# A hybrid Hyena, attention and expert block on one core: the conditioning with its weights as stationary operand, filter norms summed by TensorE, and x times root in place

## The chip, the core and the metric

One NeuronCore of a Trainium2 chip, one launch. The metric is the device time of one execution in microseconds, as the median of several runs. The core has TensorE (PE in the profile; its weight loads are shown as PEld), VectorE (DVE), ScalarE (ACT), GpSimd (POOL) and SyncE (SP, which issues most DMAs). Each engine takes its own instructions in order.

## What is computed

All in float32, on x of 512 tokens by 1024, a context of 256 tokens, and two condition vectors c and c_ctx. Cut to what matters here:

```python
m_lat = silu(c) @ w_ada + b_ada          # 6 modules of 1024
m_ctx = silu(c_ctx) @ w_ada + b_ada
sh1, sc1, g1, sh2, sc2, g2 = m_lat       # of m_ctx only the first two are used
h = rmsnorm(x, norm1_g) * (1 + sc1) + sh1
h_ctx = rmsnorm(ctx, norm1_g) * (1 + cs1) + ch1
# hyena: two long filters, made by a small network with sines and a decay
filt = mlp(positions) * decay            # [512, order 2, forward/backward, 512]
filt = filt / sum(abs(filt))             # over positions and both directions
z = h @ w_in + b_in                      # 5120 columns: hyena 1536, q, k, v, two gates
zc = cw[0] * z[t-1] + cw[1] * z[t] + cw[2] * z[t+1] + conv_b     # the hyena columns
y_hy = hyena(zc, filt)                   # long convolutions through a Fourier transform
x1 = x + g1 * ((gate1 * (y_hy @ w_hy_out) + gate2 * (attention(h, h_ctx) @ w_na_out)) @ w_out)
out = x1 + g2 * experts(rmsnorm(x1, norm2_g) * (1 + sc2) + sh2)
```

The experts are 16384 rows of two tables, of which each token and head takes 16.

## The kernel before

The kernel is one long program written with a tile framework: the Python code gives the work in a rough order, and the framework puts each engine's instructions into a fixed order by a simulated time line. `issue_after` ties an instruction's place to another's.

Matrices whose precision matters are split into a high and a low part (`split`, L202 to L211: ACT copies the high part, DVE or GpSimd subtracts it), and each product is made of three (`mm3`, L221; `project`, L227). A product of plain float32 operands leaves two records of matmul in the trace; one of split operands leaves one.

The part that the change touches is the opening, `run`, L819 to L866:

- `conditioning` (L335) makes the first two modules (shift and scale of the first norm), for c and c_ctx at once. For each of 8 blocks of 128 inputs it loads two 128x1024 pieces of `w_ada` (L352; the first module's into the buffers of later weight splits, `wh`/`wl`, two each, the second module's into five buffers `wada`). The first module goes to TensorE with the two condition columns as the stationary operand (128x2) and 512 weight columns moving, summed in PSUM over the blocks (L347). The second module does so for blocks 5 to 7 only; for blocks 0 to 4 (SIDE = 5) DVE multiplies the piece by the condition's value of each partition and adds it to two accumulators `raw` of 128x1024 (L356, L358), which TensorE folds in at the end of block 6 by products with a column of ones (L364). The two rows of each module, over four PSUM banks of the tag "s", are copied to SBUF (L370, L371), turned into columns by 16 small transposes (L373), and the bias is added (L374); L377 makes the scale.
- `rstd` (L413) sums the squares of x (ACT squares, GpSimd adds), transposes, takes the root and spreads it back over the partitions (L403 to L419).
- `modulate` (L422) makes the normalised input: for each of 8 blocks x times root (L427), times scale plus shift (DVE L431 or ACT L429 in turns), and the split (low part on DVE or GpSimd in turns).
- `filter_mlp` (L239) is the small network; `filters` (L260) makes one long filter, for two orders, `f0` and `f1`. For each of four blocks of 128 positions: two products (L282), times decay (L284), magnitude by ACT into one of two buffers `fd` (L286), the larger of the two (L289 or L295), and, from the second block on, GpSimd adds it to `l1` (L296). In the first block, one row of the first position is added, halved and copied by DVE (L291 to L293). Then the filter is split, TensorE sums `l1` over the partitions (L304, with 128 columns of `l1` as the stationary operand and two columns of ones moving), and `spectrum` (L314) makes its transform from PSUM banks "s" (four of them). The transform's matrix `dft` (2 MB) is fetched on GpSimd's queue after the squares are summed (L841).
- `hy_block` (L487) is one block of projection and short convolution: 24 products, ACT adds the bias (L493), then DVE takes the middle tap with its bias (L494) and adds the two others (L495, L496). Four of its twelve calls are in the opening, eight in `hyena`.

Weights go through three buffers `raw`; the fetch of the first projection weights stands behind the last fetch of the conditioning (`hold`, L846). The conditioning is a generator, resumed between the steps of the filter network.

Behind the opening come the Hyena convolutions with gates (to about 300 us), attention (to about 550 us), the output projection, and the experts (routing, then all expert columns for three quarters of the tokens with a one-hot spread, and gathered rows for the others) to the end.

## Time and profile before

| | us |
|---|---|
| Median of 3 runs | 1899.73 |
| Lowest and highest run | 1883.78, 1901.09 |
| Profiled execution | 1897.7 |
| Its span, first to last instruction | 1895.9 |
| PE busy | 1818.9 (96%) |
| DVE busy | 1469.6 (78%) |
| ACT busy | 839.8 (44%) |
| POOL busy | 543.5 (29%) |
| Moved by DMA | 429.37 MB, mean 226 GB/s |

Times in the rows are microseconds from the span's start. A busy PE is not a PE at its peak: matmuls are pipelined, and the duration of one is longer than the distance to the next. The granted clock is the share of TensorE's 2.4 GHz. In a row that merges several instructions the duration runs from the first start to the last end.

### The profile page before, as it was taken

To read this page: it belongs to the slowest core of one execution; us is meant where nothing else is said; L and a number is where in the kernel's file an instruction comes from. 1 tells how busy PE (TensorE), PEld (TensorE's weight loads), DVE (VectorE), ACT (ScalarE), POOL (GpSimd) and SP (SyncE) were. 2 spreads that over 40 slices of the span, in tenths; PEclk is the share of its full clock that TensorE was granted. 3 is DMA by queue.
4 is the path that set the end of the run, shared out by engine and by line. 5 is a ranking of instruction groups with operands and counts; after the bars stand their busy time and mean duration, and the time that the engine had idled before them with its cause. 6 is when DMAs were issued, how large, how long until landed. Compare 5 with 4: busy or idle time off the path is not lost.

```text
span 1895.9 us, 26957 instructions
## 1 busy us (share of the span) xinstructions
PE 1818.9 (96%) x9939; PEld 1569.0 (83%) x9939; DVE 1469.6 (78%) x2741; ACT 839.8 (44%) x1278; POOL 543.5 (29%) x377
## 2 busy tenths in 40 slices
PE   6899999999999899999999999999999999999997
PEld 1578887878877788899998988889999999987876
DVE  7879865665788688877995768787777877778987
ACT  2553334545554543346886333333333333333332
POOL 3440000000002333340000444444444444433440
PEclk8999999999999999999999999999999999999999
DMA  8443323333477422245668979989998888889995
GB/s 306 134 164 108 123 86 120 115 110 97 133 272 239 128 84 79 79 133 190 259 263 296 320 272 331 324 305 327 323 322 301 317 318 306 302 280 333 333 329 198
DMA packets 167933, 429.37 MB, mean 226 GB/s; under 512 B 14999, under 2 KB 70487, under 8 KB 163832
## 3 DMA queue, kind: packets, MB, share of 16 engines
q1 hardware_dynamic: 127656, 280.82, 43.8%
q0 software_dynamic: 40144, 146.82, 21.2%
q8 instruction: 78, 1.28, 0.3%
q14 instruction: 55, 0.45, 0.1%
HBM read 387.22 MB, written 38.27 MB: 224 GB/s over the span
## 4 chain that ended last, share of the span: by engine, by line
PE 67%; DVE 13%; DMA 8%; issue 6%; POOL 2%; ACT 2%; SPq 1%; ACTq 0%; DVEq 0%; POOLq 0%
PE a L233 26%; PE a L235 13%; PE s L223 5%; PE s L224 5%; PE s L225 5%; POOL row L1282 2%; PE t L225 2%; PE t L223 2%; PE t L224 2%; DMA row<-in_u_rows,ei 2%; DMA raw<-in_v_rows 1%; DMA wada<-in_w_ada 1%; DMA row<-in_v_rows,ei 1%; PE s L1268 1%; PE s L1269 1%
## 5 line engine op out<-in xcount | busy, mean ns | idle before, releaser
L233 PE MATMUL a<-h,wh 128*128 128x384 f32 (+1 forms) x2944 | 613.6, 358 | 5.3 <-ACT ring L1032 1.3
L233 PEld LDWEIGHTS a<-h,wh 128*128 128x128 f32 x2944 | 524.7, 190 | 52.1 <-issue 1.9
L204 ACT ACTIVATE wh<-raw 128x1024 fp32r<-128x1024 f32 (+1 forms) x208 | 213.7, 1027 | 369.6 <-DMA raw<-in_u_cols 180.8
L235 PE MATMUL a<-h,wl 128*128 128x384 f32 (+1 forms) x1472 | 318.5, 354 | 0.0
L1282 POOL DMA_INDIRECT row<-in_u_rows,ei x128 | 186.1, 1454 | 403.1 <-DVE row L1287 387.0
L235 PEld LDWEIGHTS a<-h,wl 128*128 128x128 f32 x1472 | 261.6, 188 | 17.5
L205 DVE TENSOR_TENSOR wl<-raw,wh 128x1024 fp32r<-128x1024 f32 (+1 forms) x173 | 203.5, 1176 | 75.7 <-ACT wh L204 37.1
L1282 POOL DMA_INDIRECT row<-in_v_rows,ei x128 | 185.0, 1445 | 246.5 <-DVE h2n L1296 217.7
L1287 DVE SCALAR_TENSOR_TENSOR row<-row,h2n 128x1024 f32<-128x1024 f32 x128 | 154.9, 1222 | 69.7 <-DMA row<-in_u_rows,ei 69.5
L224 PE MATMUL s<-vl,wsh 128*128 128x512 f32 x512 | 200.8, 393 | 7.1 <-DVE vl L205 6.9
L225 PE MATMUL s<-vh,wsl 128*128 128x512 f32 x512 | 198.9, 391 | 0.0
L204 ACT ACTIVATE wsh<-w 128x384 fp32r<-128x384 f32 x128 | 67.0, 523 | 267.6 <-PE t L224 156.1
L223 PE MATMUL s<-vh,wsh 128*128 128x512 f32 x512 | 176.4, 391 | 6.1 <-ACT vh L204 3.0
L1296 DVE SCALAR_TENSOR_TENSOR h2n<-row,dots,h2n 128x1024 f32<-128x1024 f32 x127 | 162.6, 1281 | 19.5 <-DMA row<-in_v_rows,ei 18.7
L205 DVE TENSOR_TENSOR vl<-raw,vh 128x1024 fp32r<-128x1024 f32 x128 | 156.1, 1220 | 8.3 <-ACT vh L204 8.3
L204 ACT ACTIVATE vh<-raw 128x1024 fp32r<-128x1024 f32 x128 | 134.6, 1052 | 39.0 <-DMA raw<-in_v_rows 33.2
L443 POOL DMA_DIRECT2D yv<-in_w_ada x32 | 17.2, 536 | 380.8 <-DVE yv L453 165.2
L205 POOL TENSOR_TENSOR wl<-raw,wh 128x1024 fp32r<-128x1024 f32 x35 | 85.0, 2431 | 124.9 <-PE a L235 116.5
L224 PEld LDWEIGHTS s<-vl,wsh 128*128 128x128 f32 x512 | 96.6, 189 | 28.0 <-DVE vl L205 10.9
L223 PEld LDWEIGHTS s<-vh,wsh 128*128 128x128 f32 x512 | 95.8, 188 | 24.8 <-ACT vh L204 4.8
L205 DVE TENSOR_TENSOR wsl<-w,wsh 128x384 fp32r<-128x384 f32 x128 | 71.1, 555 | 55.8 <-ACT wsh L204 53.7
L225 PEld LDWEIGHTS s<-vh,wsl 128*128 128x128 f32 x512 | 96.8, 189 | 19.8
(361 smaller groups left out, 2982.2 us busy)
## 6 DMA issues: line engine op xcount, KB each, us to landing
raw<-in_u_cols SPq DMA_DIRECT2D x128, 512.0 KB
raw<-in_v_rows SPq DMA_DIRECT2D x128, 512.0 KB
Gd<-st SPq DMA_DIRECT2D x24, 1024.0 KB
G<-Gd SPq DMA_DIRECT2D x16, 1536.0 KB
raw<-in_w_in SPq DMA_DIRECT2D x40, 512.0 KB
yv<-in_w_ada POOLq DMA_DIRECT2D x32, 256.0 KB, 3.1
adaw<-in_w_ada SPq DMA_DIRECT2D x16, 512.0 KB
raw<-in_w_q SPq DMA_DIRECT2D x16, 512.0 KB
```

The lines of the kernel that those rows point to most:

```text
L204: return (nc.scalar.activation(hi, src, AF.Copy).ins, (nc.vector if eng == "v" else nc.gpsimd).tensor_tensor(lo, src, hi, ALU.subtract).ins)
L205: (nc.vector if eng == "v" else nc.gpsimd).tensor_tensor(lo, src, hi, ALU.subtract).ins)
L223: t.matmul(out, a[0], b[0], start=start, stop=False)
L224: t.matmul(out, a[0], b[1], start=False, stop=False)
L225: return t.matmul(out, a[1], b[0], start=False, stop=stop).ins
L233: t.matmul(out, w[0][:, c, :], h[x][:, c, :], start=(c == 0 and x == 0), stop=False)
L235: i = t.matmul(out, w[1][:, c, :], h[0][:, c, :], start=False, stop=(c == n - 1))
L1268: nc.tensor.matmul(p[:, t, :], eq[1][:, x, :], gh[:, x, :], start=True, stop=False)
L1269: mm = nc.tensor.matmul(p[:, t, :], eq[1][:, x, :], gl[:, x, :], start=False, stop=True).ins
L1282: nc.gpsimd.indirect_dma_start(out=r, out_offset=None, in_=self.A[tab], in_offset=bass.IndirectOffsetOnAxis(ap=ei[:, n:n + 1], axis=0))
L1287: V.scalar_tensor_tensor(r, r, 1.0, h2n, op0=ALU.mult, op1=ALU.mult, accum_out=dots[:, n:n + 1])
L1296: V.scalar_tensor_tensor(acc, r, dots[:, n:n + 1], acc, op0=ALU.mult, op1=ALU.add)
```

## The change

`conditioning`: TensorE now takes both modules in all 8 blocks, with 128x128 pieces of the weights as the stationary operand and the two condition columns moving. Each product writes its own two columns of one PSUM bank (8 blocks x 2 modules x 8 pieces x 2), without summing; one reduction on DVE adds the eight blocks, and the bias is added in place. The accumulators, the rows, their copies and the transposes go; `wada` has three buffers.

`filters`: ACT takes the magnitudes into one buffer `fd` and a slice of `l1`, which now has four slices; DVE takes the larger of the two, into the slice. TensorE makes 16 products in place of 4, one for each slice and block of columns, and DVE adds the four. The halving and the copy of the one row go to ACT. The two sums of the last network layer's weights share the one buffer.

`modulate`: for the latent tokens (`own=True`) the eight products x times root are written over x, in a loop ahead of the rest; for the context nothing changes.

`hy_block`: the middle tap goes to ACT.

```diff
-SIDE = 5
...
-            fs = self.t(fp, "fd", [64, 512], bufs=2)
+            fs = self.t(fp, "fd", [64, 512])
...
-        l1 = self.t(fp, "l1", [128, 512])
+        l1 = self.t(fp, "l1", [128, 4, 512])
         for tb in range(4):
             decay = self.load(fp, "decay", src=self.A["decay"][:, tb, :], bufs=2)
-            ab = []
             for cs in range(2):
...
-                f = fil[:, cs, tb, :]
-                nc.vector.tensor_tensor(f, p, decay, ALU.mult)
-                af = self.t(fp, "fd", [128, 512], bufs=2)
-                nc.scalar.activation(af, f, AF.Abs)
-                ab.append(af)
+                nc.vector.tensor_tensor(fil[:, cs, tb, :], p, decay, ALU.mult)
+            ab = [self.t(fp, "fd", [128, 512]), l1[:, tb, :]]
+            for cs in range(2):
+                nc.scalar.activation(ab[cs], fil[:, cs, tb, :], AF.Abs)
+            nc.vector.tensor_tensor(ab[1], ab[0], ab[1], ALU.max)
             if tb == 0:
-                nc.vector.tensor_tensor(l1, ab[0], ab[1], ALU.max)
                 a, b = fil[0:1, 0, 0, :], fil[0:1, 1, 0, :]
                 nc.vector.tensor_tensor(a, a, b, ALU.add)
-                nc.vector.tensor_scalar(a, a, 0.5, None, op0=ALU.mult)
-                nc.vector.tensor_copy(b, a)
-            else:
-                nc.vector.tensor_tensor(ab[0], ab[0], ab[1], ALU.max)
-                nc.gpsimd.tensor_tensor(l1, l1, ab[0], ALU.add)
+                nc.scalar.activation(b, a, AF.Copy, scale=0.5)
+                nc.scalar.activation(a, a, AF.Copy, scale=0.5)
...
-                pn = self.ps("t", 128, 4, 2)
-                for cb in range(4):
-                    nc.tensor.matmul(pn[:, cb, :], l1[:, cb * 128:cb * 128 + 128], self.ones[:, :2], start=True, stop=True)
+                pn = self.ps("t", 128, 4, 4, 2)
+                for tb in range(4):
+                    for cb in range(4):
+                        nc.tensor.matmul(pn[:, tb, cb, :], l1[:, tb, cb * 128:cb * 128 + 128], self.ones[:, :2], start=True, stop=True)
...
-                nc.vector.reciprocal(rn, pn[:, :, 0])
+                nc.vector.tensor_reduce(rn, pn[:, :, :, 0].rearrange("p t c -> p c t"), axis=AX.X, op=ALU.add)
+                nc.vector.reciprocal(rn, rn)
...
-        p = [[self.ps("s", 2, 512) for _ in range(2)] for _ in range(2)]
-        acc = [self.t(self.wp, "raw", [128, 1024], F32, 3) for _ in range(2)]
...
+        p = self.ps("s", 128, 8, 2, 8, 2)
         for db in range(8):
-            w = [..., self.t(wp, "wada", [128, 1024], bufs=5)]
+            w = [..., self.t(wp, "wada", [128, 1024], bufs=3)]
             for m in (1, 0):
                 i = nc.sync.dma_start(w[m], self.A["w_ada"][db * 128:db * 128 + 128, m * D:m * D + D])
...
+            for x in (1, 0):
+                for j in range(8):
+                    nc.tensor.matmul(p[:, db, x, j, :], w[x][:, j * 128:j * 128 + 128], sc[:, db, :], start=True, stop=True)
             yield i.ins
...
+        nc.vector.tensor_reduce(m, p.rearrange("p d x j v -> p (x j) v d"), axis=AX.X, op=ALU.add)
+        nc.vector.tensor_tensor(m, m, self.bada[:, :16].unsqueeze(2).to_broadcast([128, 16, 2]), ALU.add)
...
-    def modulate(self, pool, h, xT, a, b, r, bufs=2):
+    def modulate(self, pool, h, xT, a, b, r, bufs=2, own=False):
...
+        rx = [xT[:, db, :] if own else None for db in range(8)]
+        for db in range(8):
+            if own:
+                nc.vector.tensor_tensor(rx[db], r, xT[:, db, :], ALU.mult)
         for db in range(8):
             t = self.t(pool, "md", [128, n], bufs=bufs)
-            nc.vector.tensor_tensor(t, r, xT[:, db, :], ALU.mult)
+            if not own:
+                rx[db] = t
+                nc.vector.tensor_tensor(t, r, xT[:, db, :], ALU.mult)
...
-        nc.vector.tensor_scalar(o, z[:, 1:513], cw[:, blk, 1:2], cw[:, blk, 3:4], op0=ALU.mult, op1=ALU.add)
+        nc.scalar.activation(o, z[:, 1:513], AF.Identity, bias=cw[:, blk, 3:4], scale=cw[:, blk, 1:2])
```

## Rows read from the trace of the kernel before

**Rows 1.** Section 2 of the page: busy tenths of PE and the DMA engines in 40 equal slices of 47.4 us each.

```profile
PE   6899999999999899999999999999999999999997
...
DMA  8443323333477422245668979989998888889995
```

**Rows 2.** Busy time of each engine in stretches of the span: from and to, length, then busy us and records of PE, PE's weight loads, DVE, ACT and POOL, then the granted TensorE clock (1.00 is 2.4 GHz), the mean busy share of the 16 DMA engines, and GB/s.

```profile
0.00:13.80 13.80, 3.92 (x5) 0.59 (x6) 5.57 (x12) 4.01 (x7) 1.63 (x6) 1.00 0.70 269
13.80:50.00 36.20, 28.21 (x57) 5.48 (x58) 28.49 (x33) 9.52 (x14) 14.91 (x7) 0.86 0.94 311
50.00:119.20 69.20, 59.91 (x238) 39.99 (x236) 61.68 (x98) 41.28 (x72) 36.81 (x25) 0.95 0.34 107
119.20:250.00 130.80, 130.80 (x710) 112.19 (x711) 106.33 (x202) 52.94 (x87) 5.27 (x8) 1.00 0.41 141
```

**Rows 3.** The same view in stretches of 4 us in the opening (the last is 2 us).

```profile
20.00:24.00 4.00, 1.15 (x3) 0.30 (x4) 3.96 (x3) 0.63 (x1) 3.84 (x3) 0.95 0.91 286
24.00:28.00 4.00, 3.98 (x6) 0.30 (x4) 4.00 (x5) 0.00 (x0) 4.00 (x1) 0.62 1.04 308
...
32.00:36.00 4.00, 4.00 (x8) 1.04 (x9) 3.61 (x6) 0.73 (x2) 0.00 (x0) 0.50 1.10 441
...
44.00:48.00 4.00, 4.00 (x13) 0.98 (x12) 1.58 (x3) 0.60 (x1) 0.00 (x0) 1.00 0.94 254
48.00:50.00 2.00, 2.00 (x7) 0.70 (x6) 0.00 (x0) 0.00 (x0) 0.00 (x0) 1.00 0.32 129
```

**Rows 4.** PE's timeline in the opening: start, duration until the end of the last of the records, line, operation, output and inputs, shapes, number of records merged in the row; in brackets the idle time before it and what ended it.

```profile
13.78 3.36 PE L347 MATMUL s<-wh,silu_c 128*2 128x512 f32 x4 [0.90 <-DMA wh<-in_w_ada]
...
22.85 2.84 PE L347 MATMUL s<-wh,silu_c 128*2 128x512 f32 x4 [4.00 <-DMA wh<-in_w_ada]
...
41.69 3.60 PE L347 MATMUL s<-raw,one 128*2 128x512 f32 x8
...
52.62 1.88 PE L347 MATMUL s<-wl,silu_c 128*2 128x512 f32 x4
```

**Rows 5.** Timelines of PE and DVE where the result of the conditioning is put together.

```profile
63.94 1.15 PE L373 MATMUL t<-ident,wh 2*128 2x2 f32 x16
...
66.35 0.18 DVE L374 TENSOR_TENSOR mod<-t,b_ada 128x32 f32<-128x32 f32 x1
```

**Rows 6.** Timeline of the weight loads of TensorE (PEld): two groups of 128x128 transposes in the opening, and the filter norm, in which 128x128 values are the stationary operand and two columns move.

```profile
33.73 0.71 PEld L403 LDWEIGHTS t<-ident,sqs 128*128 128x128 f32 x4 [1.61 <-issue]
...
45.21 0.41 PEld L410 LDWEIGHTS a<-ident,rs 128*128 128x128 f32 x4 [0.86 <-DVE fhsl L205]
...
76.93 0.97 PEld L304 LDWEIGHTS t<-ones,l 128*128 128x128 f32 x8 [0.45 <-POOL l L296]
```

**Rows 7.** Groups of PE's instructions between 13.8 and 50 us by line: output and inputs, shapes, records | busy us, mean ns of one | idle time before them and what ended it.

```profile
L246 PE MATMUL t<-feats,f 64*64 64x512 f32 x2 | 2.0, 1084 | 3.6 <-ACT feats L256 3.6
L403 PE MATMUL t<-ident,sqs 128*128 128x128 f32 x4 | 1.1, 434 | 0.0
L410 PE MATMUL a<-ident,rs 128*128 128x128 f32 x4 | 0.7, 285 | 0.0
```

**Rows 8.** DVE's timeline in the opening: the first and the last of five pairs of multiply-adds of the conditioning (ten instructions).

```profile
12.58 3.20 DVE L356 TENSOR_SCALAR raw<-wada,silu_c 128x1024 f32<-128x1024 f32 x2 [2.44 <-DMA wada<-in_w_ada]
...
30.98 2.46 DVE L358 SCALAR_TENSOR_TENSOR raw<-wada,silu_c,raw 128x1024 f32<-128x1024 f32 x2
```

**Rows 9.** Groups of DVE's instructions between 50 and 119 us, same columns as rows 7.

```profile
L284 DVE TENSOR_TENSOR fil<-t,decay 128x512 f32<-128x512 f32 x16 | 10.7, 682 | 4.4 <-PE t L225 4.0 <-DMA decay<-in_decay 0.4
L295 DVE TENSOR_TENSOR fd<-fd,fd 128x512 f32<-128x512 f32 x6 | 6.9, 1148 | 1.2 <-ACT fd L286 1.2
...
L427 DVE TENSOR_TENSOR md<-rb,xT 128x512 f32<-128x512 f32 x6 | 4.0, 672 | 0.0
...
L494 DVE TENSOR_SCALAR yv<-zpad,cw 128x512 f32<-128x512 f32 x2 | 1.5, 745 | 0.0
L289 DVE TENSOR_TENSOR l<-fd,fd 128x512 f32<-128x512 f32 x2 | 1.3, 674 | 0.0
...
L371 DVE COPY wh<-s 2x512 f32<-2x512 f32 x2 | 1.3, 672 | 0.0
...
L293 DVE COPY fil<-fil 1x512 f32<-1x512 f32 x2 | 0.8, 408 | 0.0
L292 DVE TENSOR_SCALAR fil<-fil 1x512 f32<-1x512 f32 x2 | 0.8, 408 | 0.0
```

**Rows 10.** A reduction on DVE in the same answer.

```profile
L405 DVE TENSOR_REDUCE rs<-t 128x2 f32<-128x256 f32 x1 | 0.4, 425 | 1.1 <-PE t L403 1.1
```

**Rows 11.** A group of GpSimd's instructions between 50 and 119.2 us.

```profile
L296 POOL TENSOR_TENSOR l<-l,fd 128x512 f32<-128x512 f32 x6 | 11.3, 1889 | 3.9 <-DVE fd L295 3.9
```

**Rows 12.** Groups of PE's instructions between 50 and 119.2 us.

```profile
L304 PE MATMUL t<-ones,l 128*128 128x2 f32 x16 | 2.0, 247 | 0.0
L347 PE MATMUL s<-wl,silu_c 128*2 128x512 f32 x4 | 1.9, 592 | 0.0
L347 PE MATMUL s<-wh,silu_c 128*2 128x512 f32 x4 | 1.9, 592 | 0.0
```

**Rows 13.** The chain of work that ended last, in order of time: start, us, engine, output, line, number of records.

```profile
119.58 3.73 PE a L233 x16
```

More of the change, by code (lines that the diff above doesn't have):

```diff
@@ L338, in conditioning @@
         sc = self.silu
-        p = [[self.ps("s", 2, 512) for _ in range(2)] for _ in range(2)]
-        acc = [self.t(self.wp, "raw", [128, 1024], F32, 3) for _ in range(2)]
-        one = self.t(wp, "one", [128, 3])
-        nc.vector.memset(one, 0.0)
-        nc.vector.memset(one[:, 1:2], 1.0)
-        def rows(m, c, w, start, stop):
-            for g in range(2):
-                nc.tensor.matmul(p[m][g], c, w[:, g * 512:g * 512 + 512], start=start, stop=stop)
+        p = self.ps("s", 128, 8, 2, 8, 2)
@@ L349, in conditioning @@
         for db in range(8):
-            w = [self.t(self.wp, "wl" if db % 2 else "wh", [128, 1024], bufs=2), self.t(wp, "wada", [128, 1024], bufs=5)]
+            w = [self.t(self.wp, "wl" if db % 2 else "wh", [128, 1024], bufs=2), self.t(wp, "wada", [128, 1024], bufs=3)]
             for m in (1, 0):
                 i = nc.sync.dma_start(w[m], self.A["w_ada"][db * 128:db * 128 + 128, m * D:m * D + D])
-            if db < SIDE:
-                for v in range(2):
-                    if db == 0:
-                        nc.vector.tensor_scalar(acc[v], w[1], sc[:, db, v:v + 1], None, op0=ALU.mult)
-                    else:
-                        nc.vector.scalar_tensor_tensor(acc[v], w[1], sc[:, db, v:v + 1], acc[v], op0=ALU.mult, op1=ALU.add)
-            else:
-                rows(1, sc[:, db, :], w[1], db == SIDE, db == 7)
@@ L361, in conditioning @@
-            rows(0, sc[:, db, :], w[0], db == 0, db == 7)
-            if db == 6:
-                for v in range(2):
-                    rows(1, one[:, 1 - v:3 - v], acc[v], False, False)
+            for x in (1, 0):
+                for j in range(8):
+                    nc.tensor.matmul(p[:, db, x, j, :], w[x][:, j * 128:j * 128 + 128], sc[:, db, :], start=True, stop=True)
             yield i.ins
         m = k.tile([128, 16, 2], F32, name="mod12")
-        pt = self.ps("t", 128, 16, 2)
@@ L368, in conditioning @@
-        for x in range(2):
-            row = self.t(self.wp, "wh", [2, 1024], bufs=2)
-            nc.scalar.activation(row[:, :512], p[x][0], AF.Copy)
-            nc.vector.tensor_copy(row[:, 512:], p[x][1])
-            for j in range(8):
-                nc.tensor.transpose(pt[:, 8 * x + j, :], row[:, j * 128:j * 128 + 128], self.ident[:2, :2])
-        nc.vector.tensor_tensor(m, pt, self.bada[:, :16].unsqueeze(2).to_broadcast([128, 16, 2]), ALU.add)
+        nc.vector.tensor_reduce(m, p.rearrange("p d x j v -> p (x j) v d"), axis=AX.X, op=ALU.add)
@@ L420, in rstd @@
         return o
[L422 removed]
+    def modulate(self, pool, h, xT, a, b, r, bufs=2, own=False):
         nc = self.nc
         n = xT.shape[-1]
+        rx = [xT[:, db, :] if own else None for db in range(8)]
+        for db in range(8):
+            if own:
+                nc.vector.tensor_tensor(rx[db], r, xT[:, db, :], ALU.mult)
         for db in range(8):
             t = self.t(pool, "md", [128, n], bufs=bufs)
[L427 removed]
+            if not own:
+                rx[db] = t
+                nc.vector.tensor_tensor(t, r, xT[:, db, :], ALU.mult)
             if db % 2:
[L429 removed]
+                nc.scalar.activation(t, rx[db], AF.Identity, bias=b[:, db:db + 1], scale=a[:, db:db + 1])
             else:
[L431 removed]
+                nc.vector.tensor_scalar(t, rx[db], a[:, db:db + 1], b[:, db:db + 1], op0=ALU.mult, op1=ALU.add)
             self.split_into(h[0][:, db, :], h[1][:, db, :], t, "p" if db % 2 else "v")
@@ L846, in run @@
                 self.hold = steps[-1]
-                self.modulate(xp, self.h, xT, self.a1[:, :, 0], self.sh1[:, :, 0], r)
+                self.modulate(xp, self.h, xT, self.a1[:, :, 0], self.sh1[:, :, 0], r, own=True)
             hst2 = ExitStack()
```

2 lines of the change are left out of this document (removed).

## Prediction

> **What bounds the kernel now.** I read the clock and span first, then the 40 slices, then busy time by stage, then the timelines of the opening, last the groups of instructions of one stretch. The slices [rows 1] show PE at 6 tenths in the first slice, 8 in the second and 9 nearly everywhere behind them, so time has to be saved where PE is not yet full: in the first slices. The stages [rows 2] say it sharper. Up to 13.8 us PE has almost nothing to do. From 13.8 to 50 us the DMA engines are 94% busy at 311 GB/s and PE waits for weights. From 50 to 119.2 us DMA is down to 0.34, PE is busy 59.9 of 69.2 us at a granted clock of 0.95, and DVE is busy 61.7 us, the highest of the engines. From 119.2 to 250 us PE is busy every microsecond. So the kernel opens with a DMA-bound stage, goes through a stage in which DVE and PE hand work to each other with DVE the fuller, and is PE-bound after that. What the change gains or loses is how much earlier or later that solid PE stretch begins; behind 119.2 us I carry the shift through unchanged.
>
> The reader is to see in the fine stretches [rows 3] that transfers run near 1.0 until 48 us and then stop, and that the granted clock is 0.62 at 24 to 28 us and 0.50 at 32 to 36 us, both right behind stretches in which PE did little (1.15 of 4 us at 20 to 24 us). In the PE timeline [rows 4] the conditioning starts at 13.78 us, waits for weights at 22.85 us, and its last product runs at 52.62 us. Its result is late beyond that: the 16 small transposes of its two rows run at 63.94 us, because PE takes instructions in order and the first filter's spectra stand ahead of them, and the shift exists at 66.35 us, the scale right behind it [rows 5]. Normalised input, and with it the first projection, can't start before.
>
> **The conditioning on PE.** Before, 26 products of a two-column stationary operand with 512 columns; each leaves two records, 0.45 us a record by the row of eight in 3.60 us at full clock [rows 4]: 52 x 0.45 = 23.4 us. After, 8 x 16 products with 128x128 weights as stationary operand and two moving columns. The trace has exactly this form in the filter norm: eight records in 0.97 us of weight loads [rows 6], so 0.122 us a record, two per product. 256 x 0.122 = 31.2 us, 7.8 us more PE time, and the 1.1 us of transposes [rows 5] goes. What else PE does between 13.8 and 50 us is 2.0 us of filter network and 1.8 us of transposes [rows 7], so 13.8 + 31.2 + 3.8 = 48.8 us if PE never waits and keeps its clock. The weights come no earlier: the last transfers end near 49 us, and the projection weights and a filter load behind them (two blocks of 512 KB and 256 KB, some 5 us at 254 GB/s [rows 3]) put the last conditioning block at about 44 us, which is 4 us of products ahead of 48. I take 51 us for the end, two more for waits; bounds 48.8 and 58 (seven more, as much as PE now idles and runs slowly there).
>
> **DVE in the opening.** Ten multiply-adds of 128x1024 go away. They lie between 12.6 and 33.4 us [rows 8], under transfers that fill the engines, so I cost them at nothing of their own. What they free is order: the filter network and the root of the mean square have DVE sooner, so that eight products x times root fit before 50 us, where DVE is busy 1.6 of 6 us [rows 3]. If that cover is missing (the root is late because its transposes stand in PE's queue behind weight products), the 4.0 us below come back.
>
> **Between 50 and 119.2 us, DVE.** Six of the eight products x times root now lie here, 4.0 us [rows 9]; they move ahead of 51 us. The two row copies go: 1.3 us. Halving and copying one row of the filter goes to ACT: 1.6 us. One multiply-add of the short convolution goes to ACT: two here, 1.5 us. Ahead of that, added: one reduction of 128x256 to 32 columns, nearest row 0.425 us for 128x256 [rows 10], and two reductions of 16 columns, between nothing and the same 0.425, taken at 0.2 each: 0.85 us. The maximum of the two magnitudes is there four times per filter, as before.
>
> The sums of magnitudes leave GpSimd: six additions, 11.3 us [rows 11]. GpSimd releases 0.45 us of PE's idle time at the first norm [rows 6] and none in [rows 9], so mainly what they do to DVE counts. The same maximum takes 0.674 us in one group and 1.148 us in another [rows 9]; the difference, 6 x 0.474 = 2.8 us, is the upper bound of what goes, zero the lower, since most GpSimd work of this stretch (splits) stays. I take 1.4 us. The Trainium skill (SBUF — State Buffer, "Who interferes with whom") says that a VectorE instruction with two SBUF inputs and a GpSimd instruction that reads SBUF exclude each other for a whole instruction; by that alone all six could each hold DVE for their length, 11.3 us, and the end would be near 1880. The rows bear the effect out but not that size: six products with both inputs in SBUF kept 0.672 us on average [rows 9].
>
> DVE's sum: 4.0 + 1.3 + 1.6 + 1.5 + 1.4 - 0.85 = 9.0 us less, 52.7 instead of 61.7. With the 7.5 us in which DVE idles now kept, the stage takes 60.2 us, and 51 + 60.2 = 111.2 instead of 119.2: **8 us earlier**.
>
> **Is PE able to do that?** Of its 238 records in this stretch [rows 2] 47 are small (16 of the norms and 8 of the conditioning [rows 12], 16 transposes [rows 5], 7 other transposes); 191 have 512 columns, at 0.233 us (16 in 3.73 us [rows 13]): 44.5 us. Two filter norms with 16 products instead of 4 each cost 64 x 0.122 = 7.8 instead of 2.0 us; the conditioning's 8 records of this stretch (3.8 us [rows 12]) and the 1.1 us of transposes are gone; 0.9 us of other transposes stay. 53.2 us of work in 60.2 us: it fits, with 7 us for waits where there are 16 now. It would not fit much more, so PE is what is late next.
>
> **ACT, queues, waits.** ACT takes on two short-convolution steps here (ten more behind 119 us, where PE is full and hides them) and four one-row copies, at their price on DVE 3.1 us, beside 41.3 of 69.2 us busy [rows 2]: hidden; without the cover it is those 3.1 us. One magnitude buffer instead of two makes the first magnitude wait for the last maximum; behind it on ACT are the splits that the spectra need, at most 0.7 us a block, eight blocks, 0 to 5 us, taken as 0 since ACT waits here anyway. Three weight buffers instead of five for the second module: the transfers stand in SP's queue behind the products that free a buffer. While PE keeps up nothing is lost. The accumulators no longer hold two of the three raw buffers, so the first projection weights are fetched without waiting for the conditioning's end; and three of four PSUM banks are free for the first filter. No step behind 250 us is touched.
>
> **The rivals.** (a) The PE time isn't hidden. It has 7.8 us more in the opening and 5.8 us more in the norms. For: 48.8 us has no room for waits. Against: PE waits for weights now and would have them ready. Conditioning at 58, the rest as above: 118.2 us, 1 us gained, 1897. (b) More moves forward than was asked: with DVE free and PSUM banks free, the first filter's products and maxima (half of 10.7 and of 8.2 us [rows 9], 9.4 us) also go ahead of 51 us. Against: PE is full there, and the filter network needs it. 8 + 9.4 = 17 us, 1880. (c) The slower one: PE runs the conditioning at its lower clock. Two moving columns per weight load may not hold the clock up, and PE still waits for each weight block. For: PE granted only 0.50 to 0.62 here twice [rows 3], and a weight load of the same shape took 0.18 us at half clock against 0.10 at full [rows 6]. Against: the clock was 1.00 from 40 us on, when PE no longer paused. Doubled, 256 x 0.244 = 62.5 us, ending at 80.1; of the 60.2 us behind it, the first filter's 9.4 us can be done meanwhile: 130.9, 12 us slower, 1909; if it can't, 21 us slower, 1919; I take 1914. It decides from a spacing of about 0.135 us a record, where 32 records take as long as one weight block takes to arrive (seven in the 30.2 us from 13.8 to 44). The Trainium skill (TensorE: Matmul & The Clock Gate, "HAM oscillation — how this bites in real kernels") says that thin products that wait for a transfer at every step of the contraction fall back to half clock each time; the trace agrees for the two stretches named, and by that rule it would be (c).
>
> **How the numbers follow.** The profiled execution took 1897.7 us around a span of 1895.9; 8 off is 1889.7, and the median of the runs lies 2.0 above the profiled execution, with one run at 1883.8. I say 1890. Chances: forecast 0.45, (a) 0.22, (b) 0.17, (c) 0.16. The range, 1874 to 1912, takes in (a), (b) with the lower of the runs shown, and the lesser half of (c). A measurement of this kernel tells a difference of about 1% (19 us) from none: faster by more needs 1881 or less, which is half of (b) and a sixth of the forecast, 0.17; slower by more is the worse half of (c), 0.07; 0.76 between.
>
> **What would show it.** Right: conditioning's products spaced near 0.12 us with the clock at 1.00, shift and scale at 51 to 53 us, all x-times-root products before them, DVE about 53 us busy from there to the solid stretch, which begins near 111 us. Wrong: weight products at 0.2 us and more (c), shift and scale after 58 us (a), the first filter's products before 45 us (b), or a solid stretch that begins at 111 us with an end that doesn't move: then the shift isn't carried.

## The result and the profile after

| | before | after |
|---|---|---|
| Median of 6 runs each, us | 1897.15 | 1921.66 |
| Lowest and highest run | 1883.78, 1902.07 | 1916.29, 1925.54 |
| Profiled execution, us | 1897.7 | 1921.93 |
| Its span, us | 1895.9 | 1920.2 |

The ratio of after to before is 1.0138, with an interval of 1.01 to 1.0175: slower by 1.4%. The forecast was 1890 and a range up to 1912. It was wrong in its sign. Of the kernels in the experiments below, the profiled execution was the slowest of the runs in x1, x2, y3 and z3 and the fastest in x3, y1, w4 and v1.

Section 2 of the page after, answering to [rows 1] (PE's line): PE is now full in the first slices, yet the kernel takes longer, so PE does more work there or does it more slowly.

```profile
PE   8999998999999999999999999999999999999998
```

Busy time by stage, same stretches and columns as [rows 2]:

```profile
13.80:50.00 36.20, 36.20 (x165) 34.57 (x165) 14.57 (x20) 9.12 (x14) 8.91 (x7) 1.00 0.90 311
50.00:119.20 69.20, 68.65 (x274) 54.02 (x273) 46.42 (x75) 35.45 (x62) 17.67 (x16) 1.00 0.27 88
119.20:250.00 130.80, 128.63 (x669) 108.74 (x669) 95.88 (x184) 59.95 (x97) 10.18 (x11) 0.96 0.38 128
```

In 13.8 to 50 us PE was busy 28.21 us before and is busy all 36.20 now, without a wait for weights; DVE fell from 28.49 to 14.57. The granted clock reads 1.00, and here this column misleads. PE's timeline, where [rows 4, 6] showed the old products and the norm:

```profile
12.46 3.57 PE L341 MATMUL s<-silu_c,wada 128*128 128x2 f32 x16
15.89 3.55 PE L341 MATMUL s<-silu_c,wh 128*128 128x2 f32 x16
...
39.85 1.97 PE L244 MATMUL t<-feats,f 64*64 64x512 f32 x2
41.75 1.11 PE L374 MATMUL t<-ident,sqs 128*128 128x128 f32 x4
...
81.62 0.62 PE L222 MATMUL t<-f4sl,fhsh 64*128 64x512 f32 x1
82.04 0.62 PE L223 MATMUL t<-f4sh,fhsl 64*128 64x512 f32 x1
82.60 1.01 PE L341 MATMUL s<-silu_c,wl 128*128 128x2 f32 x4
...
86.87 0.39 PE L223 MATMUL s<-fdsh,dft 128*128 128x512 f32 x1
87.10 0.39 PE L221 MATMUL s<-fdsh,dft 128*128 128x512 f32 x1
...
124.10 2.73 PE L298 MATMUL t<-ones,l 128*128 128x2 f32 x24
...
129.04 1.70 PE L298 MATMUL t<-ones,l 128*128 128x2 f32 x8
130.60 0.77 PE L221 MATMUL s<-fdsh,dft 128*128 128x512 f32 x1
...
136.49 3.98 PE L231 MATMUL a<-h,wh 128*128 128x512 f32 x16
```

Sixteen records of the conditioning start every 3.43 us (12.46 to 15.89): 0.214 us a record, where the same form takes 0.114 us at 124.10 (24 in 2.73). A product of 512 columns starts 0.42 us behind the one before it at 82 us and 0.23 us at 87. So PE ran at half its clock, 1.2 GHz, until 86.7 us. The trace's first clock entry is the rise there; what lies before a first entry is shown as 1.00. In the kernel before the first rise stands at 16.8 us.

The first solid run of projections, at 119.58 us before [rows 13], starts at 136.49. DVE's timeline, answering to [rows 5, 9, 10]: the products x times root come at 50.28 us, the reduction at 83.65, the shift at 85.12 where it was at 66.35.

```profile
50.28 4.89 DVE L400 TENSOR_TENSOR xT<-rb,xT 128x512 f32<-128x512 f32 x8
...
83.65 0.42 DVE L344 TENSOR_REDUCE mod<-s 128x32 f32<-128x256 f32 x1 [0.25 <-PE s L341]
...
85.12 0.19 DVE L345 TENSOR_TENSOR mod<-mod,b_ada 128x32 f32<-128x32 f32 x1
```

The clock falls again behind the second burst of norm products (124.10 above), here in stretches of 4 us (the lower level lasts from 127.6 to 134.5 us):

```profile
124.00:128.00 4.00, 4.00 (x32) 3.77 (x31) 3.29 (x4) 1.76 (x4) 2.14 (x2) 0.95 0.00 0
128.00:132.00 4.00, 4.00 (x14) 3.45 (x14) 3.34 (x9) 2.86 (x5) 1.03 (x1) 0.50 0.00 0
```

**Where the time is.** I added up PE's busy time by group, overlaps counted once, from the start to the first transposes of attention's exponentials (321.1 us before, 352.3 after: 31.2 later). The conditioning grew from 28.6 to 54.9 us, the norms from 1.8 to 7.5, the filters' last layer, which now ran partly at half clock, from 14.4 to 19.2, the inverse transform from 23.4 to 26.2, everything else by 2.5: 42.1 us more. PE's idle time fell from 30.4 to 19.5, so 10.9 of it was hidden. From there to the end, the kernel after is 6.9 us shorter, which leaves the 24.3 us between the spans. Put by place instead of by kind of work, the solid run of projections starts some 17 us later, and from its start to attention the Hyena convolutions take 14 us longer, although of their code only the engine of the middle tap changed:

```profile
119.34:321.07 201.73, 198.53 (x1106) 168.94 (x1105) 148.62 (x278) 83.48 (x139) 6.35 (x10) 1.00 0.38 126
136.49:352.26 215.77, 205.46 (x1116) 174.38 (x1113) 144.46 (x270) 91.68 (x151) 6.97 (x10) 0.98 0.36 118
```

(The first row is of before, the second of after.) The delay of the start and the longer stage turn out to be two different effects.

### The profile page after: what moved, and what is told of

The parts are those of the page before. It is cut to its first block, busy times and chain, and to the rows that moved or that the text cites. A ratio compares the mean times of both kernels' runs of the same rounds, so it can differ in the third digit from the quotient of the medians.

```text
span 1920.2 us, 27408 instructions
## 1 busy us (share of the span) xinstructions
PE 1858.7 (97%) x10175; PEld 1633.5 (85%) x10175; DVE 1445.1 (75%) x2714; ACT 851.2 (44%) x1292; POOL 524.1 (27%) x371
## 4 chain that ended last, share of the span: by engine, by line
PE 77%; DVE 11%; DMA 5%; issue 3%; ACT 2%; POOL 1%; SPq 0%; DVEq 0%; ACTq 0%; POOLq 0%
PE a L231 27%; PE a L233 13%; PE s L221 6%; PE s L222 6%; PE s L223 6%; PE t L221 3%; PE t L223 3%; PE t L222 3%; PE s L341 3%; DMA row<-in_u_rows,ei 2%; DMA raw<-in_v_rows 1%; PE s L1246 1%; PE s L1247 1%; PE a L731 1%; POOL row L1260 1%
## 5 line engine op out<-in xcount | busy, mean ns | idle before, releaser
L1274 DVE SCALAR_TENSOR_TENSOR h2n<-row,dots,h2n 128x1024 f32<-128x1024 f32 x127 | 162.6, 1280 | 19.2 <-DMA row<-in_v_rows,ei 18.8
```

Of the source, the lines that this page charges most:

```text
L1274: V.scalar_tensor_tensor(acc, r, dots[:, n:n + 1], acc, op0=ALU.mult, op1=ALU.add)
```

## The experiments

Theory C: the conditioning's products leave PE at half clock. Theory N: the norm products, and the clock behind them, cost too. Rivals: the other edits of the filter code, the tap on ACT, the modulation in place, or the order of work in itself. The table is to be read with the sections below it. For the profiled execution it has when the conditioning's result is first written, when the last split of the normalised input ends, how long the stage of the convolutions takes (from the first solid run of projections behind the second filter's norms to attention), when attention starts (the first transposes of its exponentials) and how long it takes to the last of them. The code of the convolutions and of attention is the same in all, but for the middle tap and w4's edit. Then come the median of the runs and the ratio of their time to that of the kernel before, run in turns on the same chip. Medians of different rows come from different chips, so the ratios decide. "Wide" is 128 moving columns in the conditioning.

| kernel | result at | last split | convolutions take | attention at | its length | median us | ratio, interval |
|---|---|---|---|---|---|---|---|
| before | 66.4 | 94.3 | 201.7 | 321.1 | 209.2 | | 1 |
| after | 83.6 | 100.8 | 215.8 | 352.3 | 210.4 | 1921.66 | 1.0138, 1.01 to 1.0175 |
| x1 after, old conditioning | 69.4 | 89.2 | 214.1 | 334.0 | 215.3 | 1910.85 | 1.0075, 1.005 to 1.0101 |
| x2 before, new conditioning | 83.9 | 113.1 | 203.9 | 345.3 | 214.3 | 1923.8 | 1.0134, 1.0101 to 1.0167 |
| x4 after, wide | 60.7 | 82.8 | 219.1 | 332.8 | 211.8 | 1911.7 | 1.0093, 1.0065 to 1.012 |
| y3 x4, old filter code | 60.5 | 86.0 | 203.1 | 315.7 | 214.6 | 1886.47 | 0.9934, 0.9909 to 0.9959 |
| v1 after, old filter code | 83.9 | 104.6 | 203.5 | 338.5 | 216.7 | 1920.14 | 1.0162, 1.0127 to 1.0197 |
| w1 x4, sums on GpSimd | 55.9 | 78.9 | 202.0 | 309.2 | 216.6 | 1891.0 | 1.0007, 0.9984 to 1.003 |
| y4 x4, wide norms | 59.4 | 84.3 | 202.0 | 315.1 | 216.6 | 1895.66 | 1.0004, 0.998 to 1.0029 |
| y1 before, new filter code | 65.1 | 91.8 | 205.6 | 323.0 | 215.7 | 1906.2 | 1.0051, 1.002 to 1.0081 |
| z3 before, wide | 60.4 | 96.3 | 205.4 | 326.6 | 216.8 | 1907.84 | 1.0047, 1.003 to 1.0064 |
| w4 x4, see there | 60.8 | 82.8 | 218.0 | 329.3 | 211.6 | 1905.0 | 1.007, 1.005 to 1.0089 |

### The two halves of the change apart: x1 and x2

x1 has `conditioning` of before in the kernel after (with four weight buffers `wada`); x2 has `conditioning` of after in the kernel before.

```diff
 x1: after                              x2: before
-    p = self.ps("s", 128, 8, 2, 8, 2)  -    p = [[self.ps("s", 2, 512) ...
+    p = [[self.ps("s", 2, 512) ...     +    p = self.ps("s", 128, 8, 2, 8, 2)
```

> The changed kernel with the conditioning of before (rows on PE, sums on DVE; its weight buffers four instead of five, for space); filter norms, magnitudes, x times root in place and the tap on ACT as changed. Theory C (the clock): the weight products hold TensorE at its lower clock and that alone makes the change slow, so this kernel loses the 24 us and keeps what the other edits bring: 1882 to 1898 us. Rival N (the other edits): one magnitude buffer, ACT's extra work and the 32 norm products per filter make the opening long, so it stays slow: 1910 to 1922 us.

> The kernel before with the conditioning of the change alone. Theory C: conditioning records again 0.21 us apart, shift and scale after 75 us, 1912 to 1930 us. Rival N: the conditioning is not what costs, records may be slow but under transfers: 1890 to 1902 us.

x2 took 1923.8 us, all of the slowdown, with the same spacing (PE's timeline):

```profile
12.62 3.57 PE L346 MATMUL s<-silu_c,wada 128*128 128x2 f32 x16
16.05 3.55 PE L346 MATMUL s<-silu_c,wh 128*128 128x2 f32 x16
```

The conditioning suffices. But x1, without it, took 1910.85, in the range of rival N, so the other edits cost 0.75% by themselves. The table shows where: in x1 the convolutions take 214.1 us instead of 201.7, and in x2 203.9.

### The clock in the conditioning: x3 and x4

The condition vector is repeated to 64 or 128 columns (`scw`), and each product moves them all, writing past its own two columns into those that later products overwrite. Nothing is left out, and TensorE does more.

```diff
+        scw = self.t(wp, "scw", [128, 8, N])
+        nc.scalar.activation(scw..., sc.unsqueeze(2).to_broadcast([128, 8, N // 2, 2]), AF.Copy)
-   nc.tensor.matmul(p[:, db, x, j, :], w[x][:, ...], sc[:, db, :], ...)
+   nc.tensor.matmul(p[:, at:at + N], w[x][:, ...], scw[:, db, :], ...)
```

> The changed kernel, but each weight product moves 64 columns (the two condition columns, 32 times over); only the first two stay, the others are overwritten by the next products. Output as before. Theory C: more columns per weight load can raise the clock; then the records come 0.12 to 0.13 us apart, shift and scale near 52 us and 1880 to 1895 us in all. If 64 columns don't raise it, 0.21 us and 1918 to 1926 us. Rival L (the weight load of float32 data that a DMA has just written is slow by itself, whatever the clock): 0.21 us a record and 1918 to 1926 us, and dense products of the filter among them would be fast, 0.23 us for 512 columns, which in the changed kernel they are not.

> The same with 128 moving columns. Theory C: the stream is about as long as the weight load; if the clock rises 0.12 to 0.16 us a record and 1882 to 1900 us; if the clock stays low 0.21 to 0.32 us and 1920 to 1945 us. Rival L: at least 0.21 us a record, 1918 us or more.

PE's timeline of x3 (64 columns, 1924.68 us, ratio 1.016, 1.0134 to 1.0185):

```profile
12.53 3.67 PE L344 MATMUL s<-scw,wada 128*128 128x64 f32 x16
15.99 3.62 PE L344 MATMUL s<-scw,wh 128*128 128x64 f32 x16
```

and of x4 (128 columns):

```profile
12.42 3.78 PE L344 MATMUL s<-scw,wada 128*128 128x128 f32 x16
15.99 2.17 PE L344 MATMUL s<-scw,wh 128*128 128x128 f32 x16
17.99 1.95 PE L344 MATMUL s<-scw,wada 128*128 128x128 f32 x16
...
29.11 2.92 PE L344 MATMUL s<-scw,wada 128*128 128x128 f32 x16 [2.18 <-DMA wada<-in_w_ada]
```

With 64 columns nothing changes: 16 records in 3.46 us (12.53 to 15.99). With 128 the first rise of the clock stands at 16.4 us, 16 records take 2.00 us (15.99 to 17.99) and then less, PE waits for weights as the prediction had it, and the result is written at 60.7 instead of 83.6 us. More work made it faster: that the conditioning's products run at half clock, and what that delays, is shown. The time, 1911.7, lies outside both ranges named for x4. It is only 10 us below that of after, since the second cause is still in x4, whose convolutions take 219.1 us.

### The second cause: y1, y2, y3, z3

y1 is before with the filter code of after; y2 is before with x times root in place and the tap on ACT; y3 is x4 with the filter code of before; z3 is before with the wide conditioning alone. Each takes whole functions, so the diff is that of the change, cut to `filters`, to `modulate` and `hy_block`, or to `conditioning` as in x4 (y1, like x1, has four buffers `wada`).

> The kernel before with the changed filter generation alone (magnitudes kept per row block, 32 norm products by TensorE, one scratch buffer, ScalarE's scaled copies; the conditioning has one weight buffer less). Theory N (the second cause, besides the conditioning's clock, is the filter edit: bursts of norm products after which the granted clock is at its lower level for 7 to 10 us, and its longer chain of one scratch buffer): 1905 to 1912, with the clock at its lower level behind both bursts and the first K load some 8 us later than the 133 us of before. Theory O (the second cause is the tap on ScalarE or the modulation in place): 1890 to 1899, within 0.3% of before. Theory S (any shift of the second filter's spectra past the projections makes its K store, the inverse matrices and the projection weights collide): slow only if the last spectrum of the second filter ends later than 126 us.

> The kernel before with x times root in place and the middle tap of the short convolution on ScalarE, conditioning and filters as before. Theory N: 1886 to 1898, no slower than before, since neither norms nor conditioning change. Theory O: 1905 to 1912, with ScalarE the last releaser of TensorE in the projections of 120 to 300 us. Theory S: as N, unless the second filter's spectra shift.

> The changed kernel with 128 moving columns in the conditioning's products (which took it to 1911.7) and with the filter generation of before. Theory N: 1885 to 1898, the second cause is gone. Theory O: 1905 to 1913, no change against 1911.7.

> The kernel before with the new conditioning at 128 moving columns as its only edit. Clock theory: products at 0.112 us each from 16 us on, result at about 61 us against 66.4 us before, and 1882 to 1897 in all, against 1923.8 with two moving columns. A rival (the conditioning on TensorE costs by its work and not by its clock: it delays filter products and moves the order of work): 1903 to 1915 although the result comes at 61 us.

y2 took 1898.28 us, ratio 1.0005 (0.9983 to 1.0027): those two edits cost nothing, and gain nothing there. y1 is 0.5% slower, as theory N expected. N had wrong that its first K load comes later than before and that the clock falls behind both bursts of norm products (only behind the second). y3 is 0.7% faster than before: the filter code is the second cause. It costs 25 us by the medians, 1.6% by the ratios, where the opening is otherwise fast (y3 to x4). z3 came out slower, as its rival said: its result is 6 us earlier than before and its last split 2 us later. That is taken up last.

### What in the filter code: w1 and y4, and the conditioning again: v1

w1 keeps the new filter code but sums on GpSimd, with 8 norm records; y4 keeps the 32 records and moves 128 columns of ones; v1 is the kernel after with the old filter code.

```diff
 w1
+            if tb:
+                nc.gpsimd.tensor_tensor(l1, l1, ab[1], ALU.add)
...
 y4
-    nc.tensor.matmul(pn[:, tb, cb, :], l1[...], self.ones[:, :2], ...)
+    nc.tensor.matmul(pn[:, at:at + 128], l1[...], self.ones[:, :128], ...)
```

> The changed kernel with 128 moving columns in the conditioning (1911.7) in which GpSimd adds the magnitudes of the four row blocks as before and TensorE sums 4 column blocks (8 records) where it had 16 (32 records); the other edits of the filter code (one scratch buffer, halving and copy on ScalarE) stay. Theory N1 (the norm products are what the filter edit costs): 1884 to 1898, as with the filter code of before (1886.5). Theory N2 (the scratch buffer and ScalarE's part are): 1905 to 1914.

> As the kernel of 1911.7, with 128 moving columns of ones in the norm products too. Theory clock (the fall of the granted clock behind each burst of norm products with 2 moving columns is what they cost beyond their own time): no lower clock right behind 98 us, and 1895 to 1904. Theory work (their own 7.7 us on TensorE, and where they shift the order of the work to, are the cost): 1907 to 1915, clock or not.

> The changed kernel, its conditioning as it is (2 moving columns), with the filter code of before. Clock theory (the conditioning on TensorE at its lower clock is a cause of its own, with 20.9 us more busy time than with 128 columns, of which the opening hides a part): 1896 to 1912, against 1886.5 with 128 columns and 1921.7 with the new filter code. A rival (only the two together are slow): 1884 to 1892.

x4 behind its second burst of norm products (98.11 us), by stretches (columns as in [rows 2]):

```profile
100.00:104.00 4.00, 3.18 (x16) 2.28 (x15) 3.96 (x7) 2.06 (x5) 2.54 (x3) 0.72 0.00 0
104.00:108.00 4.00, 3.54 (x12) 3.20 (x13) 3.60 (x10) 1.50 (x2) 1.53 (x1) 0.50 0.00 0
108.00:112.00 4.00, 4.00 (x11) 3.09 (x10) 0.00 (x0) 0.00 (x0) 0.00 (x0) 0.50 0.00 0
```

y4, the same view: the clock is 1.00 right behind its burst (96.49 us), and falls only behind a stretch in which PE works 1.16 of 4 us.

```profile
100.00:104.00 4.00, 1.16 (x6) 0.45 (x4) 4.00 (x5) 3.00 (x4) 3.82 (x3) 1.00 0.00 0
104.00:108.00 4.00, 3.58 (x14) 3.09 (x15) 3.56 (x10) 0.30 (x1) 0.00 (x0) 0.62 0.00 0
```

In x4 the clock is at its lower level for 10.2 us (101.8 to 112.0), in which PE is busy 3.18 to 4.00 of each 4 us; in y4 for 3.4 us. y4 took 1895.66 us, 16 less than x4, though its norms have the same records, and that was the range of the clock theory. w1 took 1891.0, with one scratch buffer and ACT's part in place, so these two are not what costs most.

But the clock behind the burst is not what y4 saves. The solid run of projections starts at 113.71 us in x4 and at 113.14 in y4, 0.57 us apart. The difference arises behind it, from there to attention (x4, then y4):

```profile
113.71:332.79 219.08, 205.98 (x1114) 174.80 (x1112) 144.72 (x270) 91.22 (x151) 8.14 (x10) 0.97 0.36 116
113.14:315.10 201.96, 198.67 (x1107) 168.89 (x1105) 144.33 (x269) 91.19 (x150) 8.15 (x10) 1.00 0.39 126
```

PE idles 13.1 us in x4 and 3.3 in y4, and spends 13.7 us at the lower clock there and none in y4. What differs is the order of PE's work, which the framework sets anew for each kernel. In x4 the last spectra of the second filter stand behind the start of the solid run, and a wait of 4.29 us comes in the convolutions; in y4 the spectra stand ahead and no such wait comes (x4, then y4):

```profile
125.93 0.40 PE L223 MATMUL s<-fdsh,dft 128*128 128x512 f32 x1
...
272.81 0.58 PE L221 MATMUL s<-idft,Yqh 128*128 128x256 f32 x1 [4.29 <-ACT Yqh L202]
```

```profile
112.54 0.40 PE L223 MATMUL s<-fdsh,dft 128*128 128x512 f32 x1
...
113.14 3.97 PE L231 MATMUL a<-h,wh 128*128 128x512 f32 x16
```

The other traces agree. Spectra behind the start of the solid run, and this wait, are found in after, x1, x3, x4 and w4, whose convolutions take 213 to 219 us, and in no other kernel, where they take 202 to 206. Record for record, and the spectra aside, after, x1, x4 and w4 have the same order of PE there. So the rival "order of work in itself" accounts for most of what the filter code costs up to attention, 11 to 17 us in that stage against before. y4, which has the other order with every norm record in place, shows that it isn't the norms' own time on PE (7.7 us in x4, 7.9 in y4). No run varies the order alone; what tips the framework's choice, and why this order waits, is open. Nor do the ratios close: w1 and y4 lie 0.7% above y3, though w1's attention starts 6.5 us earlier than y3's.

v1 answers for the conditioning in the whole: 1920.14 us, 8 more than the clock theory allowed, against 1886.47 of y3. The sources of the two differ in the moving columns of the conditioning alone (the framework's order ahead of the solid run differs with them). The result is written 23.3 us later and attention starts 22.8 us later (338.5 against 315.7), with convolutions of nearly the same length. That is the larger cause. With the conditioning at half clock the filter edit no longer shows at the end: v1 and after have overlapping intervals, though after's attention starts 13.8 us later still. Its attention is 6.3 us shorter; the other 4.6 us come back behind attention, and which work gives them back is open.

### A collision of transfers: w4

In x4 PE also stands still at 139 us, for 4.95 us, and the clock falls behind it (PE's timeline, then a stretch):

```profile
144.08 6.46 PE L231 MATMUL a<-h,wh 128*128 128x512 f32 x16 [4.95 <-ACT gz L578]
```

```profile
144.00:148.00 4.00, 3.92 (x9) 3.14 (x10) 2.24 (x6) 1.88 (x5) 0.00 (x0) 0.50 0.92 343
```

The second filter's store, the inverse matrices, a filter load and the projection weights fill the DMA engines together, since the last spectra ended at 126.3 us, behind the first projections. w4 was to fetch the inverse matrices later.

```diff
-        with self.tc.issue_after(self.low):
-            for x in range(2):
-                for cs in range(2):
-                    nc.gpsimd.dma_start(idft[:, x, cs], self.A["idft"][:, x, cs])
-        yield from self.hy_spectra(0, 1, y, dft, hp, Y)
+        for step, _ in enumerate(self.hy_spectra(0, 1, y, dft, hp, Y)):
+            if step == 0:
+                ...                      # the same fetches, behind the last split of hy_spectra
+            yield
```

> As the kernel of 1911.7, with the inverse matrices (2.1 MB) fetched later, behind the transposes of the second half of the first convolution, so that they no longer stand beside the second filter's K store and the projection weights. Theory S (this burst starves TensorE at 139 to 144 us, and the clock falls behind the gap, together 8 us): no gap there, and 1901 to 1906. Theory work: 1908 to 1914, the gap goes or moves and the time stays.

The gap stayed, 4.72 us ahead of 141.45, and the ratio, 1.007 (1.005 to 1.0089), overlaps that of x4. The median lies in the range of theory S, but not for its reason, since the edit moved nothing. GpSimd's timeline, of x4 and then of w4, has the fetches at the same place, 1.1 us behind the end of the last spectra (126.33 and 123.93 us):

```profile
127.42 2.18 POOL L555 DMA_DIRECT2D idft<-in_idft  x4 [0.31 <-POOL hc L203]
```

```profile
125.02 2.18 POOL L558 DMA_DIRECT2D idft<-in_idft  x4 [0.31 <-POOL hc L203]
```

So which transfer starves PE is open, the inverse matrices not excepted. What w4 does show is a second execution of x4's order of work up to the gap, with the clock at its full level behind the second burst of norm products (x4 has 0.57 in this stretch):

```profile
100.00:112.00 12.00, 10.62 (x65) 9.13 (x65) 8.85 (x20) 5.68 (x11) 4.39 (x4) 1.00 0.00 0
```

Its solid run starts 2.4 us earlier than x4's and its attention 3.5, where y4's starts 17.7 earlier. That again puts the larger part on the order and not on the clock behind the burst.

### Whether the predicted gain is real: z4 and z5

z4 and z5 add to z3 one edit each: x times root in place, and the tap on ACT.

> The kernel before with the new conditioning at 128 moving columns (1907.8 by itself) and x times root in place, the middle tap still on VectorE. Theory P (the prediction's own step: the eight products of x times root go into VectorE's idle time ahead of the conditioning's result, and the last split of the normalised input comes about 10 us earlier): last split by 88 us and 1884 to 1893. Theory T (the tap on ScalarE is what pays, by freeing VectorE in the projections): 1902 to 1910.

> The kernel before with the new conditioning at 128 moving columns (1907.8 by itself) and the middle tap on ScalarE, x times root as before. Theory P: last split of the normalised input at 93 us or later and 1902 to 1910. Theory T: 1884 to 1893.

z4 took 1897.66 (1.0009, 0.9992 to 1.0026) and z5 1896.99 (1.0003, 0.9984 to 1.0023), by the ratios each 0.4% less than z3, and y3 with both another 0.7% below. Both lie between the ranges of the two theories: neither alone, both edits pay. DVE's timeline of z3 and then of z4 shows the first:

```profile
34.28 1.28 DVE L408 TENSOR_TENSOR md<-rb,xT 128x512 f32<-128x512 f32 x2
69.65 0.68 DVE L408 TENSOR_TENSOR md<-rb,xT 128x512 f32<-128x512 f32 x1
...
87.52 1.27 DVE L408 TENSOR_TENSOR md<-rb,xT 128x512 f32<-128x512 f32 x2
```

```profile
34.27 4.89 DVE L410 TENSOR_TENSOR xT<-rb,xT 128x512 f32<-128x512 f32 x8
```

All eight products stand ahead of the result, and the last split ends at 86.4 instead of 96.3 us; attention starts 7.5 us earlier (319.1 against 326.6): the solid run 4.8 us earlier, and convolutions of 202.8 instead of 205.4 us. With z5 the last split stays (95.8) and attention starts 4.8 us earlier (321.8), 3.5 of them in the convolutions (201.9 us); its other 7 us are in attention, 209.5 against 216.8 us, in code that the edit doesn't touch. That part of the tap's gain isn't shown to be the tap's. And z3 and y1, the two kernels that are half a per cent slower than before, share nearly one order of PE in the convolutions, which no other has, so the part in that stage goes with the order too.

## Why the prediction was wrong, step by step

- **PE keeps its clock (256 x 0.122 = 31.2 us, end at 51 us): the step that failed.** The price came from eight norm records that stood between spectra at full clock [rows 6]. Measured: 0.214 us, 54.9 us, the last products at 82.60. That is 26.3 us more than the old form took; part of it filled idle time, and the solid stretch began 16.9 us later than before instead of 8 earlier. x2 shows that this suffices for the slowdown, x4 that the clock is the reason for the spacing.
- **Rival (c)** had the mechanism and put it at 1909 to 1919 with a chance of 0.16. Its size was near, in part by luck: 0.244 us forecast for 0.214, 80.1 us for the end and 83.6 measured, since 12 us of filter products came in between. Of its two reasons the first, that two moving columns may not hold the clock up, fits; the second, that PE waits for each weight block, didn't happen. PE did not wait once (36.20 of 36.20 us busy, above), and neither did it in x3 (37.40 of 37.40 us from 12.6 to 50). The Trainium skill (TensorE: Matmul & The Clock Gate, "HAM oscillation — how this bites in real kernels") explains thin products at half clock by waits for transfers; its outcome agrees with the trace, and that cause doesn't, since here the half clock is there without a wait.
- **The evidence for and against (c)** was misread. "The clock was 1.00 from 40 us on" described PE with 512 moving columns in nearly every record. What spoke for (c) was in the rows: 0.18 us for a weight load at half clock [rows 6], nearly the spacing that came.
- **Weights arrive by 44 us and are the limit**: true only in the wide form, where PE waits for them again (29.11 above).
- **Eight products x times root before 50 us**: they came at 50.28, the lost cover that the text named, since the third layer of the small network (39.85) and the root's transposes (41.75) stood in PE's queue behind weight products. It cost nothing while the result was later still. In the wide form they stand at 34 us, and z4 shows the gain.
- **DVE 9.0 us less, so the solid stretch 8 us earlier**: right in kind. With the conditioning at full clock and the old norms, y3, attention starts 5.4 us earlier than before and the time is 0.66% lower, some 12 us. That this is close to what was forecast for the whole change is luck in part, since y3 has none of the filter edits.
- **Sums of magnitudes cost DVE 1.4 us, bounds 0 and 2.8**: the maximum takes 0.685 us after (seven) where six took 1.148 [rows 9]. But in w1, with five of GpSimd's sums in the same stretch, it takes 0.754 (five). So the sums were not what stretched it. Before, each of the four slow maxima began while GpSimd ran a split or added squares, and ended 0.55 us behind that one's end; none met a sum. The sums held two other instructions of DVE, for some 1.8 us in all, the second shown below: the 1.4 us were near by luck. The Trainium skill (SBUF — State Buffer, "Who interferes with whom") says that a VectorE instruction with two inputs in SBUF contends with a GpSimd instruction that reads SBUF. The traces agree where the two met. That each sum would hold DVE for its length isn't what came, since most met no such instruction that began behind them.

```profile
L284 DVE TENSOR_TENSOR l<-fd,l 128x512 f32<-128x512 f32 x7 | 4.8, 685 | 0.9 <-ACT l L283 0.7
```

```profile
L284 DVE TENSOR_TENSOR mg<-fd,mg 128x512 f32<-128x512 f32 x5 | 3.8, 754 | 0.2 <-ACT mg L283 0.2
...
L286 POOL TENSOR_TENSOR l<-l,mg 128x512 f32<-128x512 f32 x5 | 8.1, 1629 | 6.0 <-DVE mg L284 4.1 <-DVE mod L350 1.9
```

The two groups above are of after and of w1. Before, a sum (GpSimd's timeline) and the instruction that it held (DVE's):

```profile
105.40 1.46 POOL L296 TENSOR_TENSOR l<-l,fd 128x512 f32<-128x512 f32 x1
```

```profile
105.76 1.66 DVE L495 SCALAR_TENSOR_TENSOR yv<-zpad,cw,yv 128x512 f32<-128x512 f32 x1
```

- **Norms 7.8 instead of 2.0 us**: 7.5 and 1.8 measured. The size was right, and what came with them was left out: the order of the spectra behind them, and the lower clock behind the burst.
- **ACT hides what it takes on**: y2 and z5 agree.
- **The shift is carried through unchanged**: the second step that failed. Behind the start of the solid stretch the convolutions, put into another order, take 14.0 us longer (215.77 against 201.73). Attention, unchanged, takes 209.2 to 216.8 us among these kernels, a spread of 7.6 us, nearly as much as the 8 us that were forecast.

## What to carry to other kernels

Price an instruction from rows whose surroundings are those that it will have: the same form cost 0.114 us among wide products and 0.214 us among its own kind. When a change puts a long run of narrow products on TensorE, compare the spacing of a known wide product behind it (0.42 against 0.23 us here), not the clock column alone. Before moving sums from an engine with slack to TensorE, look at which engine is full in the next stage; here both moves put work on the engine that sets the end. And where a framework orders the work, compare the order of two kernels behind the edit before putting a difference down to the edit itself: y4 came out in the range of a theory whose mechanism was worth little.

## What the runs showed of the hardware

- In after and x3 PE ran at 1.2 GHz for some 70 us while it was busy without a wait (2 and 64 moving columns, a median of 0.213 us from one record to the next in both). In x4, with 128 columns, it was at 2.4 GHz from 16.4 us to the end of the conditioning, but for 3.4 us behind the wait for weights at 29 us. 64 columns instead of 2 cost 1.0 us of PE time (54.9 to 55.9), and 128 instead of 2 saved 20.7 (54.9 to 34.2).
- Behind or in bursts of 24 to 32 narrow norm products the clock fell to its lower level, for 3.4 to 10.2 us, in 8 of 12 cases: at both bursts in x1 and x3, at the second alone in after, x4 and y1, at the first alone in w4. In x3 PE did not wait at all from 12 to 140 us. x4 and w4 issue the same products in the same order, so a burst alone doesn't tell whether the clock falls; what else decides is open.
- Attention, the same code in all, takes 209.2 to 216.8 us and spends 6.8 to 17 us at the lower clock. The two go together only in part: 209.2 us with 6.8 (before) and 214.5 to 216.8 with 17 (x1, y3, w1, y4, v1, z3), but 210.4 (after) and 215.7 (y1) with the same 13.7.
- In before, four of DVE's maxima of two SBUF operands began while GpSimd ran a subtraction or an addition. They ended 0.55 us behind it and took 1.2 to 1.8 us; the other four took 0.67 to 0.68.
